# Weight preparation in half pieces, q written per half block, and the first attention block's loads moved: a two-layer streaming encoder on one core

## The chip, the core and the metric

The kernel runs on one core of a Trainium2 chip. The metric is the device time of one execution, in microseconds (us). The core has a matrix engine (TensorE, PE in the rows, with its weight loads as PEld), a vector engine (VectorE, DVE), an activation engine (ScalarE, ACT), a general engine (GpSimd, POOL) and a queue engine (SyncE, SP) that issues nearly all transfers. Each engine takes its instructions in the order in which they stand in its own queue, so an instruction that waits holds back all that stand behind it.

## What is computed

One inference step over 4096 prompt rows and 64 sample rows of width 1024: a gated convolution layer, then one shared key/value projection, then chunk-banded attention with sinks, each with RMS norms and residuals. Cut to what matters:

```python
# layer 0: z = rmsnorm(x) @ w_in + b; u = a * sigmoid(gl); c = depthwise conv31(u)
#          x1 = x + rmsnorm((silu(layernorm(c)) * silu(gate)) @ w_out + b_out)
kv = rmsnorm(x1, kv_g) @ w_kv                    # 2 heads of 64 for K and for V
z = rmsnorm(x1, b_pre_g) @ b_w_in                # 1024 q columns, 1024 gate columns
o = softmax(q @ K.T / 8 - slope * dist, sink) @ V    # own chunk of 64 and the two before it
y = x1 + rmsnorm((o * silu(gate)) @ b_w_out, b_post_g)
```

Each fp32 product is made of three fp16 products (high and low parts), accumulated in PSUM.

## The kernel before, in words

The program has four stages, in order of time.

1. **Stage A** (to about 1120 us): input projections of layer 0 and the depthwise convolution, in blocks of 512 rows.
2. **Output stage** (1120 to 1545 us): the loop `for ti in range(EARLY, len(L) + 1)` calls `la_iter(ti)`, a software pipeline over 33 tiles of 128 rows: layer norm, silu, gate, 48 matmuls with `w_oa`, and the rows of x1 to the DRAM scratch `x1_scr`. The first ten iterations stand in the stage before. On odd `ti` one weight job is called: two `kv_chunk`s and four `strassen_chunk`s that prepare the weights of q (`w_q...`). From `ti` 27 on, the steps of `prep_x1` for the first two blocks of the next stage are called in between.
3. **Projection stage** (1550 to 1998 us): 17 blocks of up to 256 rows in the order 0 to 14, 16 (the sample rows), 15. `proj_qkv(b)` gives ten PE jobs: the seven Strassen products of q in 128x128 tiles (`p1` to `p7`), K, and V twice. Between them stand the nine steps of `prep_x1` of the next block: norm, transposes, split into high and low parts, sums for the Strassen products (`tTb`). `out` adds up a product of q into an fp32 tile `zq`; when both halves (`th` 0 and 1) of 256 columns are there, `put_q` scales, splits and stores them in `q_scr`. From block 7 on (`G_AT`), odd blocks call one `strassen_chunk` for the gate weights and even blocks four `put_w_ob`.
4. **Attention stage** (from 1998 us): units of (128 rows, KV head). `load_att(b)` fetches q (`qraw`, then copied to `qs` on POOL), `ks` and `v_`. `gate_jobs(b)` are the seven Strassen products of the gate, popped by `filler` between the steps of the units; those of block 0 are called whole at the end of the projection stage.

`strassen_chunk(..., i)` (L865 to L898) loads 128 rows of 2048 values in two halves, 1 MB in four transfers of 256 KB into one buffer `wst`, scales them with two activations of 1024 columns, forms S1 to S4 on POOL (512 columns, L876), and splits seven operands: an ACT copy to fp16 (L883), a DVE subtraction for the low part (L884).

The order of instructions is not that of the code alone. The `TileContext` orders each engine's queue by a simulated timeline: when an engine is free in the simulation, it takes the earliest called instruction that is ready there. So a piece of work that is called late but needs little is put ahead, as early as its buffers allow. The tile constants `bias`, `sk` and `nsk` (L1343 to L1353) are made at the start of the attention stage, in its pool `pb`, which shares memory with the projection stage's pool `p3`.

Of the kernel before, what the change touches and what calls it, by code (L numbers as in the profile page):

```python
# [60 lines left out]
G_AT = 7  # L61
# [6 lines left out]
def tile_streaming_conformer(  # L68
# [778 lines left out]
    q_scr = dpool.tile([nb, 2, 2, P, 4, TB], F16, name="q_scr")  # L847
# [14 lines left out]

    OPS = ("A11", "S1", "S2", "A12", "S3", "A22", "S4")

    def strassen_chunk(pool, dst, names, base, i):  # L865
        st = pool.tile([P, 2, D], F32, tag="st", name="wst", bufs=1)
        src = ins["b_w_in"][0].rearrange("(g h kb c) n -> g c h kb n", g=4, h=2, c=G4)
# [4 lines left out]
        v = dict(A11=st[:, 0, 0:HN], A12=st[:, 1, 0:HN], A21=st[:, 0, HN:], A22=st[:, 1, HN:])  # L872

        def comb(name, a, b, op):
            v[name] = pool.tile([P, HN], F32, tag="sw", name=f"sw_{name}", bufs=3)
            nc.gpsimd.tensor_tensor(out=v[name], in0=v[a], in1=v[b], op=op)  # L876

        def put(name):
            if name in names:
                o = dst[name][:, :, i, :]  # L880
            else:
                o = pool.tile([P, 2, HN], F16, tag="wo", name=f"wo_{name}", bufs=1)
            nc.scalar.copy(o[:, 0], v[name])  # L883
            nc.vector.tensor_tensor(out=o[:, 1], in0=v[name], in1=o[:, 0], op=ALU.subtract)  # L884
            if name not in names:
                nc.sync.dma_start(out=wg_scr[OPS.index(name) - 5, :, :, i, :], in_=o)

        put("A11")
        put("A12")
        put("A22")  # L890
        comb("S1", "A21", "A22", ALU.add)
        put("S1")
        comb("S2", "S1", "A11", ALU.subtract)
        put("S2")
        comb("S3", "A11", "A21", ALU.subtract)
        put("S3")
        comb("S4", "A12", "S2", ALU.subtract)
        put("S4")  # L898
# [195 lines left out]
    def proj_qkv(b, ht, pool):  # L1094
# [4 lines left out]
        def put_k(src, n, scale, dst, name):  # L1099
            o = pool.tile([P, 2, TB], F16, tag="ko", name=name)  # L1100
# [46 lines left out]
        def put_q(kv, src):  # L1147
            zh = pool.tile([P, 4, TB], F16, tag="qo", name=f"qh_{b}_{kv}", bufs=4)
            zl = pool.tile([P, 4, TB], F16, tag="qo", name=f"ql_{b}_{kv}", bufs=4)
            for jj in range(4):  # L1150
                scale = SQ * 2.0 ** (4 * kv + jj) / 8.0 / SP
                nc.scalar.activation(zh[:, jj, :T], src[:, jj, :], AF.Copy, scale=scale)
                nc.vector.scalar_tensor_tensor(
                    out=zl[:, jj, :T], in0=src[:, jj, :], scalar=scale, in1=zh[:, jj, :T],
                    op0=ALU.mult, op1=ALU.subtract,
                )
            for z, t in ((0, zh), (1, zl)):
                nc.sync.dma_start(out=q_scr[b, kv, z, :, :, :T], in_=t[:, :, :T])

        if samp:  # L1160

            def q_half(half):
                ps = ps_mm([P, KH, CH], f"psqs_{half}")
                samp_half(wq, hT, tT, half, ps)
                put_q(half, ps)
# [3 lines left out]
        zq = {}  # L1169

        def out(nh, th, ps, add):
            if nh not in zq:
                zq[nh] = pool.tile([P, 4, TB], F32, tag="zq", name=f"zq_{b}_{nh}")
            dst = zq[nh][:, :, th * P : th * P + P]
            if add is None:
                nc.scalar.copy(dst, ps)
            else:
                nc.vector.tensor_tensor(out=dst, in0=ps, in1=add, op=ALU.add)
            zq[nh, th] = True
            if (nh, 0) in zq and (nh, 1) in zq:  # L1180
                put_q(nh, zq[nh])
# [5 lines left out]
    with ExitStack() as ph:  # L1187
# [11 lines left out]
        def kv_chunk(k0):  # L1199
            st = pl.tile([P, 4, 2 * P], F32, tag="st", name="wst", bufs=1)  # L1200
            split_weight(w_kv, ins["w_kv"], st, list(range(k0, k0 + 4)), 0, 256, 0, 1, quads=True)

        wjobs.extend(lambda k0=k0: kv_chunk(k0) for k0 in (0, 4))
        wjobs.extend(lambda i=i: strassen_chunk(pl, wq, OPS, 0, i) for i in range(KH))

        early = deque()
        for ti in range(EARLY, len(L) + 1):
# [10 lines left out]
            if ti % 2 == 1 and wjobs:  # L1218
                wjobs.popleft()()
        while wjobs:  # L1220
            wjobs.popleft()()
# [62 lines left out]

    with ExitStack() as ph:
# [4 lines left out]
        gjobs.extend(lambda i=i: strassen_chunk(p3, wg, OPS[:5], D, i) for i in range(KH))  # L1290
        wob_v = ins["b_w_out"][0].rearrange("(k p) n -> p k n", p=P)

        def put_w_ob(g, k):
            st = p3.tile([P, HN], F32, tag="wos", name=f"wob_{g}_{k}", bufs=1)
            nc.sync.dma_start(out=st, in_=wob_v[:, k, g * HN : g * HN + HN])
            w = p3.tile([P, 2, HN], F16, tag="wow", name=f"wobs_{g}_{k}", bufs=1)
            nc.scalar.activation(w[:, 0], st, AF.Copy, scale=SW)
            nc.vector.scalar_tensor_tensor(
                out=w[:, 1], in0=st, scalar=SW, in1=w[:, 0], op0=ALU.mult, op1=ALU.subtract
            )  # L1300
            nc.sync.dma_start(out=wob_scr[k // KH * 2 + g, :, :, k % KH, :], in_=w)

        ojobs = deque(lambda g=g, k=k: put_w_ob(g, k) for g in range(2) for k in range(KB))
# [3 lines left out]
        for q_, b in enumerate(order3):  # L1307
# [23 lines left out]
        assert not gjobs and not ojobs  # L1331
# [3 lines left out]
        for _, fn in gate_jobs(0):  # L1335
            fn()
# [3 lines left out]
    with ExitStack() as ph:  # L1340
        pb = ph.enter_context(tc.tile_pool(name="pb", bufs=2, reuse_waits="tile"))

        bias = pb.tile([P, 3 * CH], F32, tag="bias", name="bias", bufs=1)  # L1343
        nc.sync.dma_start(out=bias, in_=ins["alibi"])
        sk = pb.tile([P, 2, 4], F32, tag="sk", name="sk", bufs=1)
        sinks = ins["b_sinks"][0].rearrange("(a t s) -> s a t", a=2, s=2)
        for s_ in range(2):
            nc.sync.dma_start(out=sk[s_ * 64 : s_ * 64 + 64], in_=sinks[s_].partition_broadcast(64))
        nsk = pb.tile([P, 2, 4], F32, tag="nsk", name="nsk", bufs=1)
# [351 lines left out]
```

## Time and profile before

| | us |
|---|---|
| runs (3), median | 2980.38 (2977.71 to 2984.27) |
| the profiled execution | 2980.22 |
| its span, first to last instruction | 2978.1 |
| PE busy in the span | 2812.6 (94%) |
| DVE busy | 2340.3 (79%) |
| ACT busy | 1886.2 (63%) |
| POOL busy | 1830.6 (61%) |

A busy time is a sum over instructions of one engine; the engines work side by side, so the times don't add up. What a stage costs is read where PE, the busiest engine, is idle or has a low granted clock.

### The profile page before, as it was taken

To read this page: it belongs to the slowest core of one execution; us is meant where nothing else is said; L and a number is where in the kernel's file an instruction comes from. 1 tells how busy PE (TensorE), PEld (TensorE's weight loads), DVE (VectorE), ACT (ScalarE), POOL (GpSimd) and SP (SyncE) were. 2 spreads that over 40 slices of the span, in tenths; PEclk is the share of its full clock that TensorE was granted. 3 is DMA by queue.
4 is the path that set the end of the run, shared out by engine and by line. 5 is a ranking of instruction groups with operands and counts; after the bars stand their busy time and mean duration, and the time that the engine had idled before them with its cause. 6 is when DMAs were issued, how large, how long until landed. Compare 5 with 4: busy or idle time off the path is not lost.

```text
span 2978.1 us, 63632 instructions
## 1 busy us (share of the span) xinstructions
PE 2812.6 (94%) x24441; PEld 1795.0 (60%) x24441; DVE 2340.3 (79%) x4387; ACT 1886.2 (63%) x4403; POOL 1830.6 (61%) x1867
## 2 busy tenths in 40 slices
PE   8989999999999988988997899997999999999998
PEld 5444444444444433444457899996777777777774
DVE  6999899999999999979877767735666666666665
ACT  6787776877776675456667676634555555555554
POOL 7899899998898999978635433313323333332332
PEclk9999999999999999989999999999999999999999
DMA  5311211211110125576647655556323332432321
GB/s 182 110 48 38 74 50 43 66 48 46 47 40 29 50 90 171 162 194 191 190 159 236 218 200 187 180 162 202 99 92 115 113 99 92 130 100 92 111 81 47
DMA packets 250742, 341.25 MB, mean 115 GB/s; under 512 B 38886, under 2 KB 172774, under 8 KB 249670
## 3 DMA queue, kind: packets, MB, share of 16 engines
q1 hardware_dynamic: 250437, 337.19, 35.3%
q8 instruction: 191, 3.13, 0.5%
q14 instruction: 114, 0.93, 0.1%
HBM read 206.46 MB, written 130.72 MB: 113 GB/s over the span
## 4 chain that ended last, share of the span: by engine, by line
PE 37%; DVE 5%; ACT 3%; DMA 3%; issue 1%; POOL 1%; SPq 1%; POOLq 0%; DVEq 0%; ACTq 0%
PE sx_g L904 5%; PE sx_q L904 4%; PE psy L182 4%; PE psy L179 4%; PE psy L180 4%; PE sz_g L904 3%; PE ptr L1493 3%; PE pv L1527 3%; PE sz_q L904 2%; PE sw_g L904 1%; ACT p L1458 1%; PE sc L1427 1%; PE sc L1428 1%; PE sw_q L904 1%; DVE p L1431 1%
## 5 line engine op out<-in xcount | busy, mean ns | idle before, releaser
L597 POOL TENSOR_TENSOR pacc<-pacc,pr 128x512 f32<-128x512 f32 x704 | 907.4, 1304 | 69.7 <-ACT pr L588 42.6
L611 DVE SCALAR_TENSOR_TENSOR acc<-u,pt,acc 128x512 f32<-128x512 f32 x1088 | 789.4, 750 | 17.8
L588 ACT ACTIVATE pr<-u,pt 128x512 f32<-128x512 f32 x704 | 485.0, 715 | 162.0 <-POOL pacc L597 150.0
L1458 ACT ACTIVATE p<-p,st 128x192 f32<-128x192 f32 (+1 forms) x520 | 227.8, 440 | 76.2 <-DVE st L1452 75.9
L1431 DVE CUSTOM_DVE_ANT_0 p<-sc,bias 128x192 f32<-128x192 f32 (+1 forms) x520 | 160.5, 349 | 87.0 <-PE sc L1428 64.7
L179 PE MATMUL psy<-w_oa,hl 128*128 128x512 f16 x512 | 202.0, 395 | 6.0 <-DVE xr L392 4.9
L1477 POOL TENSOR_TENSOR p<-p,st 128x768 f32<-128x768 f32 (+2 forms) x130 | 185.5, 1447 | 34.5 <-DVE st L1473 27.8
L187 PE MATMUL ps_a<-hT,w_a 128*128 128x512 f16 (+1 forms) x528 | 198.2, 375 | 5.3 <-ACT sg L680 5.0
L187 PE MATMUL ps_gl<-hT,w_gl 128*128 128x512 f16 (+1 forms) x528 | 199.3, 377 | 3.8 <-ACT sig L751 1.9
L179 PE MATMUL psy<-w_ob,ogT 128*128 128x512 f16 x512 | 195.7, 382 | 7.0 <-ACT ogT L1543 6.8
L187 PE MATMUL ps_gt<-hT,w_gt 128*128 128x512 f16 x512 | 197.0, 385 | 5.4 <-DVE u L733 5.2
L180 PE MATMUL psy<-w_oa,hl 128*128 128x512 f16 x512 | 201.0, 393 | 0.0
L188 PE MATMUL ps_gl<-hT,w_gl 128*128 128x512 f16 (+1 forms) x528 | 199.3, 377 | 0.9 <-DVE hT L206 0.9
L189 PE MATMUL ps_gl<-hT,w_gl 128*128 128x512 f16 (+1 forms) x528 | 199.0, 377 | 0.0
L188 PE MATMUL ps_a<-hT,w_a 128*128 128x512 f16 (+1 forms) x528 | 198.0, 375 | 0.0
L189 PE MATMUL ps_a<-hT,w_a 128*128 128x512 f16 (+1 forms) x528 | 198.0, 375 | 0.0
L188 PE MATMUL ps_gt<-hT,w_gt 128*128 128x512 f16 x512 | 196.9, 385 | 0.0
L189 PE MATMUL ps_gt<-hT,w_gt 128*128 128x512 f16 x512 | 196.4, 384 | 0.0
L180 PE MATMUL psy<-w_ob,ogT 128*128 128x512 f16 x512 | 195.8, 382 | 0.0
L904 PEld LDWEIGHTS <-w_gS 128*128 128x128 f16 x3072 | 181.2, 98 | 20.2 <-issue 15.2
L904 PEld LDWEIGHTS <-w_qS 128*128 128x128 f16 x3072 | 177.3, 99 | 10.9 <-issue 10.5
L1377 POOL COPY qs<-qraw 128x1024 f16<-128x1024 f16 (+1 forms) x68 | 68.5, 1034 | 171.5 <-PE sc L1428 78.6
(352 smaller groups left out, 7079.9 us busy)
## 6 DMA issues: line engine op xcount, KB each, us to landing
x<-in_x_prompt SPq DMA_DIRECT2D x32, 512.0 KB, 3.8
g_scr<-sg SPq DMA_DIRECT2D x64, 256.0 KB, 2.2
c_scr<-c SPq DMA_DIRECT2D x64, 256.0 KB, 2.0
c<-c_scr SPq DMA_DIRECT2D x32, 512.0 KB, 4.2
g<-g_scr SPq DMA_DIRECT2D x32, 512.0 KB, 4.6
x<-x_scr SPq DMA_DIRECT2D x128, 128.0 KB, 3.6
h_scr<-hTb SPq DMA_DIRECT2D x32, 512.0 KB, 3.2
h_scr<-tTb SPq DMA_DIRECT2D x32, 512.0 KB, 3.7
```

The source lines that it names most:

```text
L179: nc.tensor.matmul(out, wts[i][0], mov[i][0], start=i == 0, stop=False)
L180: nc.tensor.matmul(out, wts[i][0], mov[i][1], start=False, stop=False)
L187: nc.tensor.matmul(out, wh, mh, start=i == 0, stop=False)
L188: nc.tensor.matmul(out, wh, ml, start=False, stop=False)
L189: nc.tensor.matmul(out, wl, mh, start=False, stop=i == n - 1)
L588: nc.scalar.activation(dst[:, :T], u[:, k : k + T], AF.Identity, scale=wdw[:, j, k : k + 1], bias=pt[:, j, R_DWB : R_DWB + 1] if k == 0 el ...
L597: nc.gpsimd.tensor_tensor(out=pacc[:, :T], in0=pacc[:, :T], in1=dst[:, :T], op=ALU.add)
L611: nc.vector.scalar_tensor_tensor(out=dst[:, :T], in0=u[:, k : k + T], scalar=wdw[:, j, k : k + 1], in1=src[:, :T], op0=ALU.mult, op1=ALU.add,)
L904: nc.tensor.matmul(ps[:, j, :], w[:, wz, kb, j * P : j * P + P], rhs(rz, kb), start=first and j + kb + wz + rz == 0, stop=last and j == KH ...
L1431: nc.vector.tensor_tensor_reduce(out=pbuf[:, t, par * 192 + lo : par * 192 + 192], in0=ps[:, tt, :nk], in1=bias[:, lo:], scale=1.0, scalar ...
L1458: nc.scalar.activation(pp, pp, AF.Exp, scale=2.0 ** -(kv * 4 + t) / SQ, bias=st[:, 1, par, t : t + 1], accum_out=st[:, 3, par, t : t + 1],)
L1477: nc.gpsimd.tensor_tensor(out=pp, in0=pp, in1=st[:, 4, par, :, None].to_broadcast([P, 4, 3 * CH - lo]), op=ALU.mult)
```

## The change

- `strassen_chunk` takes half of the columns (`hc`), so there are 8 pieces instead of 4 for q and 8 instead of 4 for the gate. It returns two functions, `load` and `comp`. A load is eight transfers of 64 KB. For q (`base` 0) the activations that scale a piece are four of 256 columns, and the factor 2^j of each 128 columns is folded in there (`gq`).
- In the output stage, an iteration calls either a `load` or the `comp` of the load before, in turn, from `ti` 10 on: ten pieces take the iterations 10 to 29. In the projection stage, a load of the gate weights is called after each of the blocks 2 to 9 in order (`G_AT = 2`) and one of `w_ob` after each of the first 16; the `comp`s are called after the next block.
- `queued()` puts each instruction of a `comp` on ACT, DVE and POOL behind the last instruction that was called on that engine before.
- `out` and `put_q` work on one product of 128 rows: the sum is left in PSUM, one activation and one DVE instruction of 512 columns split it, and the stores wait for both halves as before, in another layout of `q_scr`. The tile `zq` is gone.
- `load_att`, `bias`, `sk`, `nsk`, `unsc` move to a pool `stp` that is open during the projection stage as well. `load_att(0)` is called after the sample block, one block before the stage ends; the constants are made before the stage's first block. POOL copies q in eight pieces per block, not four.
- `gate_jobs(0)` is called after the first unit's scores and softmax statistics, not before the attention stage.

```diff
-G_AT = 7
+G_AT = 2
+    def queued():
+        es = ExitStack()
+        for e in (nc.scalar, nc.vector, nc.gpsimd):
+            seen = (x for x in reversed(nc.cur_bb.bb.instructions) if x.engine == e.engine)
+            es.enter_context(tc.issue_after(next(seen)))
+        return es
-    def strassen_chunk(pool, dst, names, base, i):
-        st = pool.tile([P, 2, D], F32, tag="st", name="wst", bufs=1)
-        for g in range(4):
-            nc.sync.dma_start(out=st[g * G4 : g * G4 + G4], in_=src[g, :, :, i, base : base + D])
-        for h in range(2):
-            nc.scalar.activation(st[:, h], st[:, h], AF.Copy, scale=gsc[:, 2, KH * h + i : KH * h + i + 1])
+    def strassen_chunk(pool, dst, names, base, i, hc):
+        def load():
+            box["st"] = st = pool.tile([P, 2, 2, HC], F32, tag="st", name="wst", bufs=1)
+            for g in range(4):
+                for h in range(2):
+                    s2 = src[g, :, h, i, base : base + D].rearrange("c (m n) -> c m n", m=2)
+                    nc.sync.dma_start(
+                        out=st[g * G4 : g * G4 + G4, h], in_=s2[:, :, hc * HC : hc * HC + HC]
+                    )
...
-        def put_q(kv, src):
-            for jj in range(4):
-                scale = SQ * 2.0 ** (4 * kv + jj) / 8.0 / SP
-                nc.scalar.activation(zh[:, jj, :T], src[:, jj, :], AF.Copy, scale=scale)
-                nc.vector.scalar_tensor_tensor(
-                    out=zl[:, jj, :T], in0=src[:, jj, :], scalar=scale, in1=zh[:, jj, :T],
+        def put_q(kv, th, src):
+            scale = SQ * 2.0 ** (4 * kv) / 8.0 / SP
+            nc.scalar.activation(zh, src, AF.Copy, scale=scale)
+            nc.vector.scalar_tensor_tensor(out=zl, in0=src, scalar=scale, in1=zh, op0=ALU.mult, op1=ALU.subtract)
...
-            if add is None:
-                nc.scalar.copy(dst, ps)
-            else:
-                nc.vector.tensor_tensor(out=dst, in0=ps, in1=add, op=ALU.add)
+            src = ps
+            if add is not None:
+                src = add if (nh, th) == (1, 1) else ps
+                nc.vector.tensor_tensor(out=src, in0=ps, in1=add, op=ALU.add)
+            put_q(nh, th, src)
...
-            if ti % 2 == 1 and wjobs:
-                wjobs.popleft()()
+            if wnext:
+                with queued():
+                    wnext.pop()()
+            elif wjobs:
+                load, comp = wjobs.popleft()
+                load()
+                wnext.append(comp)
...
-            if q_ >= G_AT and q_ % 2 and gjobs:
-                gjobs.popleft()()
+            while wnext:
+                with queued():
+                    wnext.pop()()
+            for js, at in ((ojobs, 0), (gjobs, G_AT)):
+                if js and q_ >= at:
+                    load, comp = js.popleft()
+                    load()
+                    wnext.append(comp)
             if q_ == nb - 2:
+                load_att(0)
                 gate_load(0)
-            if q_ >= G_AT and q_ % 2 == 0 and ojobs:
-                for _ in range(4):
-                    ojobs.popleft()()
-        for _, fn in gate_jobs(0):
-            fn()
...
-        load_att(0)
         sc, stats = att_scores(*units[0])
         for fn in sc:
             fn()
         stats()
+        for _, fn in gate_jobs(0):
+            fn()
```

## Rows read from the trace of the kernel before

**Rows 1.** The page: PE's busy tenths in 40 slices of the span.

```profile
PE   8989999999999988988997899997999999999998
```

**Rows 2.** Four stretches: start:end, length, busy us and count per engine, clock, DMA.

```profile
1280.00:1430.00 150.00, 130.22 (x587) 61.55 (x586) 133.82 (x158) 98.29 (x204) 125.67 (x141) 0.93 0.67 188
1430.00:1500.00 70.00, 70.00 (x348) 35.13 (x346) 56.09 (x73) 42.55 (x95) 41.65 (x63) 1.00 0.61 186
1550.00:1736.00 186.00, 157.18 (x2472) 151.10 (x2473) 141.24 (x258) 129.67 (x350) 79.84 (x56) 0.95 0.68 217
1736.00:1932.00 196.00, 196.00 (x3307) 193.83 (x3305) 137.36 (x290) 136.77 (x411) 64.64 (x48) 1.00 0.53 184
```

**Rows 3.** Waits of ACT from 1280 to 1430: us in total, times, longest.

```profile
ACT w_qS L883 <- POOL sw_S L876: 12.3, 5, 4.1
ACT wst L871 <- DMA wst<-in_b_w_in: 10.7, 2, 6.5
```

**Rows 4.** Waits of ACT from 1550 to 1736.

```profile
ACT wobs L1297 <- DMA wob<-in_b_w_out: 12.7, 8, 4.8
```

**Rows 5.** DVE by line, 1280 to 1430: the subtractions of the weight jobs.

```profile
L884 DVE TENSOR_TENSOR w_qS<-sw_S,w_qS 128x512 f16<-128x512 f32 x16 | 16.1, 1015 | 0.0
L884 DVE TENSOR_TENSOR w_qA<-wst,w_qA 128x512 f16<-128x512 f32 x12 | 13.5, 1155 | 2.8 <-ACT w_qA L883 2.8
L159 DVE SCALAR_TENSOR_TENSOR w_kv<-wst,gsc,w_kv 128x256 f16<-128x256 f32 x8 | 5.5, 714 | 0.2 <-ACT w_kv L158 0.2
```

**Rows 6.** The tile wst: ns min/median/max; the last line is its transfers' landing.

```profile
L869 SPq DMA_DIRECT2D wst<-in_b_w_in x32: 323/423/798, 1301.1 to 1631.8; - x32
L871 ACT ACTIVATE wst<-wst,gsc x16: 1131/1135/1150, 1311.5 to 1639.3; 128x1024 f32<-128x1024 f32 x16
L876 POOL TENSOR_TENSOR sw_S<-wst x16: 1261/1390/1720, 1313.8 to 1643.5; 128x512 f32<-128x512 f32 x16
L883 ACT CAST w_qA<-wst x12: 600/606/618, 1314.5 to 1389.4; 128x512 f16<-128x512 f32 x12
DMA to landing us min/median/max: 2.6/5.2/10.2
```

**Rows 7.** The tile zq: the instructions that write q.

```profile
L1152 ACT ACTIVATE qh<-zq x128: 398/404/422, 1584.9 to 1997.6; 128x256 f16<-128x256 f32 x128
L1153 DVE SCALAR_TENSOR_TENSOR ql<-zq,qh x128: 410/419/1484, 1585.3 to 1998.1; 128x256 f16<-128x256 f32 x128
L1178 DVE TENSOR_TENSOR zq<-sz_q,U_q x32: 675/682/693, 1579.0 to 1995.8; 128x512 f32<-128x512 f32 x32
L1176 ACT COPY zq<-sx_q x16: 566/579/585, 1583.2 to 1993.1; 128x512 f32<-128x512 f32 x16
```

**Rows 8.** Timelines around an undisturbed block's start: start us, us, engine, line.

```profile
1806.14 2.96 DVE L1028 TENSOR_TENSOR tTb<-tf,tTb 128x256 f16<-128x256 f32 x6
...
1809.39 2.85 PE L904 MATMUL sx_q<-hTb,w_qA 128*128 128x128 f16 x48
...
1812.26 0.94 PE L904 MATMUL sz_q<-tTb,w_qS 128*128 128x128 f16 x14
```

**Rows 9.** Timelines of DVE, SP and PE at the start of attention; brackets: idle before.

```profile
1999.42 1.35 SPq L1348 DMA_DIRECT2D sk<-in_b_sinks  x2
...
2011.87 0.58 DVE L1352 TENSOR_SCALAR nsk<-sk 128x1 f32<-128x1 f32 x8 [13.35 <-DMA qraw<-q_scr]
2012.36 0.69 DVE L1274 TENSOR_TENSOR sw_g<-sw_g,P_g 128x512 f32<-128x512 f32 x1
...
2014.21 4.46 PE L904 MATMUL sx_g<-tl,w_gA 128*128 128x128 f16 x48 [7.43 <-ACT U_g L922]
...
2027.34 0.49 PE L904 MATMUL sx_g<-tl,w_gS 128*128 128x128 f16 x6 [1.23 <-DMA tl<-h_scr]
...
2034.14 4.19 PE L904 MATMUL sx_g<-tl,w_gS 128*128 128x128 f16 x43 [2.68 <-ACT U_g L922]
```

**Rows 10.** Transfers by tile: count, KB each, median us from issue to landing.

```profile
x<-x_scr SPq DMA_DIRECT2D x128, 128.0 KB, 3.6
...
wst<-in_w_kv SPq DMA_DIRECT2D x8, 128.0 KB, 8.7
```

More of the change, by code (lines that the diff above doesn't have):

```diff
@@ L861, in tile_streaming_conformer @@
         nc.gpsimd.tensor_copy(fv[:, g], fv[:, 0])
+    gq = cpool.tile([P, 4, KB], F32, name="gq")
+    for j in range(4):
+        nc.gpsimd.tensor_scalar(gq[:, j], gsc[:, 2], scalar1=2.0**j, scalar2=None, op0=ALU.mult)
     OPS = ("A11", "S1", "S2", "A12", "S3", "A22", "S4")
-    def strassen_chunk(pool, dst, names, base, i):
-        st = pool.tile([P, 2, D], F32, tag="st", name="wst", bufs=1)
-        src = ins["b_w_in"][0].rearrange("(g h kb c) n -> g c h kb n", g=4, h=2, c=G4)
-        for g in range(4):
-            nc.sync.dma_start(out=st[g * G4 : g * G4 + G4], in_=src[g, :, :, i, base : base + D])
-        for h in range(2):
-            nc.scalar.activation(st[:, h], st[:, h], AF.Copy, scale=gsc[:, 2, KH * h + i : KH * h + i + 1])
[L872 to L880, printed above, removed]
-            else:
[L882 to L898, printed above, removed]
@@ L1099, in put_k @@
         def put_k(src, n, scale, dst, name):
-            o = pool.tile([P, 2, TB], F16, tag="ko", name=name)
+            o = pool.tile([P, 2, TB], F16, tag="ko", name=name, bufs=1)
             nc.scalar.activation(o[:, 0, :n], src, AF.Copy, scale=scale)
@@ L1199, in kv_chunk, with load @@
         def kv_chunk(k0):
[L1200 to L1204, printed above, removed]
+            box = {}
+            def load():
+                st = pl.tile([P, 4, 2 * P], F32, tag="st", name="wst", bufs=1)
+                box["f"] = split_weight(
+                    w_kv, ins["w_kv"], st, list(range(k0, k0 + 4)), 0, 256, 0, 1, now=False, quads=True
+                )
+            return load, lambda: box["f"]()
+        wjobs.extend(kv_chunk(k0) for k0 in (0, 4))
+        wjobs.extend(strassen_chunk(pl, wq, OPS, 0, i, hc) for i in range(KH) for hc in range(2))
+        wnext = []
         early = deque()
@@ L1283, in tmp @@
         return stp.tile([P, KH, P], F32, tag=tag, name=name)
+    bias = stp.tile([P, 3 * CH], F32, tag="bias", name="bias", bufs=1)
+    nc.sync.dma_start(out=bias, in_=ins["alibi"])
+    sk = stp.tile([P, 2, 4], F32, tag="sk", name="sk", bufs=1)
+    sinks = ins["b_sinks"][0].rearrange("(a t s) -> s a t", a=2, s=2)
+    for s_ in range(2):
+        nc.sync.dma_start(out=sk[s_ * 64 : s_ * 64 + 64], in_=sinks[s_].partition_broadcast(64))
+    nsk = stp.tile([P, 2, 4], F32, tag="nsk", name="nsk", bufs=1)
@@ new lines, in tile_streaming_conformer, with load_v @@
+    unsc = stp.tile([P, 2, 4], F32, tag="unsc", name="unsc", bufs=1)
+    for t in range(8):
+        nc.vector.tensor_scalar_mul(nsk[:, t // 4, t % 4 : t % 4 + 1], sk[:, t // 4, t % 4 : t % 4 + 1], -SQ * 2.0**t)
+        nc.gpsimd.memset(unsc[:, t // 4, t % 4 : t % 4 + 1], 2.0**-t / SQ)
+    vt = {}
+    def load_v(key, src, n):
+        v = vt[key] = stp.tile([P, 3, 2, P], F16, tag="v", name=f"v_{key}", bufs=4)
+        nc.sync.dma_start(out=v[:n, 0], in_=src)
+        for half in range(2):
+            hs = slice(half * 64, half * 64 + 64)
+            nc.sync.dma_start(out=v[hs, 1], in_=src[0:64])
+            if n > CH:
+                nc.sync.dma_start(out=v[hs, 2], in_=src[64:128])
@@ L1341, in tile_streaming_conformer @@
         pb = ph.enter_context(tc.tile_pool(name="pb", bufs=2, reuse_waits="tile"))
[L1343 to L1349, printed above, removed]
@@ L1350, in tile_streaming_conformer @@
-        unsc = pb.tile([P, 2, 4], F32, tag="unsc", name="unsc", bufs=1)
-        for t in range(8):
-            nc.vector.tensor_scalar_mul(nsk[:, t // 4, t % 4 : t % 4 + 1], sk[:, t // 4, t % 4 : t % 4 + 1], -SQ * 2.0**t)
-            nc.gpsimd.memset(unsc[:, t // 4, t % 4 : t % 4 + 1], 2.0**-t / SQ)
-        vt, U, OG = {}, {}, {}
-        def load_v(key, src, n):
-            v = vt[key] = pb.tile([P, 3, 2, P], F16, tag="v", name=f"v_{key}", bufs=4)
-            nc.sync.dma_start(out=v[:n, 0], in_=src)
-            for half in range(2):
-                hs = slice(half * 64, half * 64 + 64)
-                nc.sync.dma_start(out=v[hs, 1], in_=src[0:64])
-                if n > CH:
-                    nc.sync.dma_start(out=v[hs, 2], in_=src[64:128])
@@ L1399, in tile_streaming_conformer @@
+        U, OG = {}, {}
         pgb = pb.tile([P, D], F32, tag="pgb", name="pgb", bufs=1)
```

176 lines of the change are left out of this document (114 added, 62 removed).

## Prediction

> **What bounds the kernel now.** I read PE's line in 40 slices first [rows 1]: beside the first and the last slices it falls below 9 in four places: slices 15 and 16 (1042 to 1191 us, before the change's first instruction), 18 and 19 (the output stage, 1266 to 1415), 22 and 23 (the projection stage's first third, 1563 to 1712) and 28 (the start of attention). Elsewhere PE is nearly full, so the last three can give time. Then I counted what the dips cost with the busy times of four stretches [rows 2], by the number of matmuls done and not by the busy share, because a matmul at the low clock also counts as busy.
>
> In the output stage the stretch without weight jobs does 348 matmuls in 70 us, 4.97 per us, at clock 1.00. The 150 us before it, in which the q weights are prepared, do 587, worth 118.1 us at that pace: **31.9 us lost**, with clock 0.93. In the projection stage the undisturbed stretch does 3307 in 196 us, 16.87 per us (eight blocks of 24.5 us); the first six blocks, where the gate weights and `w_ob` are prepared, do 2472 in 186 us, worth 146.5: **39.5 us lost**. So the weight jobs called from block 7 on run in blocks 0 to 5: they were put ahead, into places where their engines looked free. At the start of attention [rows 9] PE stands idle 7.43, 1.23 and 2.68 us, and after two of these the first group runs at half the clock: 4.46 us for 48 matmuls against 2.85 [rows 8], and 4.19 for 43 against 2.55, so 3.2 more: **14.6 us lost**. Together 86.0 us.
>
> Why PE waits there: ACT stood 10.7 us on the landing of the q weights and 12.3 us on POOL's sums [rows 3], in the projection stage 12.7 us on `w_ob` rows [rows 4], each time with the copies that PE needs queued behind. Loads and the work on them were called together; a load takes 5.2 us to land, up to 10.2 [rows 6].
>
> **The change part by part.**
>
> *Weight pieces in the output stage.* A load now has an iteration's lead. An iteration is 54 matmuls (48 with `w_oa`, six short ones), 10.9 us at 4.97 per us. Issuing eight transfers costs SP 8 x 0.423 = 3.4 us [rows 6]; with the median landing of 5.2 that is 8.6 us, inside the iteration. So ACT's wait for loads should go. What is late next is DVE. Undisturbed it is busy 56.09 of 70 us [rows 2], so it has 2.17 us free per iteration, 43 us in the 20 iterations of ten pieces. The work is 16.1 + 13.5 + 5.5 = 35.1 us [rows 5]; halving adds 28 times 2 x 0.419 - 0.682 = 0.16, 4.4 us (durations of 256 and 512 columns, [rows 7]). That makes 39.5 of 43. It fits, but with no room, and the stretch that is undisturbed now gets its share. POOL's sums stretch DVE's subtractions too (means of 1.015 and 1.155 us against 0.68 alone [rows 5, 7]), which halves don't cure. I leave half of the loss in place and take **15 us gained** (some 1.8 us lost per half piece still, 17 us in all). Bounds: a loss of 3 (the same loss, and halves dearer) to a gain of 28.
>
> *Weight pieces in the projection stage.* One gate piece per block in blocks 3 to 10, one `w_ob` piece in each. ACT: two scalings of half 1.135 and seven copies of 0.404, 4.0 us; DVE seven of 0.419, 2.9 us alone; POOL four of half 1.39, 2.8 us [rows 6, 7]. A block leaves ACT 24.5 x (1 - 136.77/196) = 7.4 us and DVE 7.3 [rows 2]. Work fits, so what counts is lateness: the pieces stand ahead of the next block's preparation. Its last subtraction ends at 1809.10 and the first matmuls that read it start at 1812.26 [rows 8], so the chain has 3.2 us to give, against 4.0. I take 1.2 us lost per gate piece (9.6) and 0.1 for each of 16 `w_ob` pieces: of 39.5, **28 us gained**, bounds 5 to 37. The loads stand in SP's queue ahead of x1 loads and q stores and wait until the piece before is read; those have a block's lead, so nothing, at most 3 us, within the bounds.
>
> *q per half block.* Per block ACT goes from 0.579 + 8 x 0.404 = 3.81 to 4 x 0.579 = 2.32 us; DVE saves 8 x 0.419 - 4 x 0.682 = 0.6 us [rows 7]. In undisturbed blocks PE is the bound and this gives nothing; in the disturbed ones it is part of the 28. A PSUM tile of a product is now held over two more instructions, 1.3 us; the pool has a third tile, and no row shows PE waiting for one. Cost nothing; without that cover 0.7 us a block, 12 in all.
>
> *Start of attention.* The 7.43 us wait goes back to DVE, which stood 13.35 us on `nsk` until the sinks landed: issued at 1999.42, `nsk` at 2011.87, 12.4 us [rows 9]. Behind it stood the sum of a gate product, behind that ACT's copy, behind that PE. With constants and q of block 0 there a block earlier, and the first unit's softmax behind the gate products, the 14.6 us should go. I take **13 us gained**: the eight loads and eight POOL copies of `load_att(0)` now stand in SP's queue ahead of the last gate weights and the last block's stores, and two of the six `big` buffers are held in block 0. Bounds 5 to 14.6.
>
> *The sinks at their new place.* The transfer is the same and still lands 12.4 us after its issue; `nsk` now waits at the start of the projection stage, where block 1's transposes and the first sums stand behind it on DVE, and the x1 loads of block 1 behind the transfer on SP's queue. No row shows how early memory is free for it. Bounds: 12.4 us lost (DVE comes to it at once) to nothing (issued two iterations earlier); I take **6 us lost**, halfway, as nothing is nearer.
>
> Sum: 15 + 28 + 13 - 6 = 50. The profiled execution took 2980.22, 2.1 over its span and 0.16 below the median of three; 2980.2 - 50 = **2930 us**.
>
> **Rivals.**
>
> *The loss goes with the work.* Each half piece costs half of what a piece cost, so the 71.4 us stay and only 13 - 6 = 7 us come: 2973 us. For it speaks that the same instructions collide with the same neighbours and that DVE has no room in the output stage; against it that 23.4 us of ACT's waits [rows 3, 4] are for loads, which now come early.
>
> *The loads come late.* 64 KB transfers could land as slowly as the slowest now: 3.4 + 10.2 = 13.6 us against an iteration of 10.9, so ACT stands 2.7 us in each of ten iterations, 27 us: 2957 us. The rows lean both ways: 128 KB of x1 land in 3.6 us, 128 KB of `w_kv` in 8.7 [rows 10]. The Trainium skill speaks against this edit (DMA: Bandwidth & Descriptors, section Bandwidth): batch transfers to 1 MiB, since small ones spend their time on descriptors; by it this rival would come first. Its figures are for another issuing path, and the x1 row doesn't bear it out.
>
> *The pieces are free.* Both stages run at their undisturbed pace: 86 - 6 = 80 us, 2900 us. DVE's 39.5 of 43 us speaks against it.
>
> *Slower.* A piece stands whole ahead of the next iteration or block, because its instructions are called earlier: ACT scales (4 x 0.404), waits for POOL's four sums (2.8) as in [rows 3], copies 0.404, DVE 0.419, 5.2 us, and 0.6 for PE's low clock after it, 5.8 us. The 80 us that can be had are used up at 5.0 us for each of 16 half pieces; at 5.8 the time is 2980 - 80 + 93 = 2993 us. Against it: an undisturbed block has 3.2 us of slack, and ACT can take other work between two copies.
>
> That the change does nothing is hardly open: the order that it forces is on the very engines that made PE wait.
>
> **How the numbers follow.** Forecast (2910 to 2955) 0.62; free 0.09; late loads 0.09; loss with the work 0.13; slower 0.07. A measurement of this kernel tells 0.2%, 6 us, from no change. Faster by more: 0.62 + 0.09 + 0.09 and half of 0.13 make 0.86; within 0.2%: 0.06; slower: 0.08. The range reaches past the free case and to just below the third rival: 2897 to 2972.
>
> **What would show it.** Right: matmuls per us near 4.7 from 1280 to 1500 and near 16 in blocks 1 to 10; no wait of ACT for `wst` or `wob`; no 7 us gap before the first gate group; the gate subtractions spread over blocks 3 to 10. Wrong: DVE idle for ten us before `nsk` around 1550 with PE idle behind it; ACT waiting for `sw_S` in every piece; a gap in front of the first scores. The prediction falls if a half piece still costs PE above 3 us, or if the wait for the sinks costs more at its new place than at its old one.

## The result, and the profile after

| | before | changed |
|---|---|---|
| median of the runs, us | 2979.98 (2977.71 to 2984.27) | 2956.06 (2950.06 to 2958.04) |
| span of the profiled execution, us | 2978.1 | 2956.3 |
| ratio of the times, 95% interval | | 0.9915 (0.9896 to 0.9933) |

The kernel is 24 us faster, inside the range and well short of the 50 us that the sum gave. The first view is the one of [rows 2] again: busy times of the same four stretches (start:end, length, busy us and count of PE, its weight loads, DVE, ACT and POOL, clock, DMA share, GB/s).

```profile
1280.00:1430.00 150.00, 139.18 (x654) 66.53 (x652) 132.04 (x172) 96.44 (x222) 116.11 (x154) 0.98 0.64 195
1430.00:1500.00 70.00, 64.98 (x314) 31.21 (x313) 60.61 (x85) 50.59 (x128) 46.72 (x69) 1.00 0.54 165
1550.00:1736.00 186.00, 172.14 (x2858) 168.84 (x2856) 124.92 (x254) 123.54 (x344) 66.44 (x62) 0.97 0.64 208
1736.00:1932.00 196.00, 187.23 (x3109) 183.00 (x3107) 139.05 (x277) 138.64 (x387) 74.77 (x64) 1.00 0.64 209
```

Against [rows 2] the first stretch does 67 matmuls more and the second 34 fewer: the pieces are spread over the whole output stage, and half of what the disturbed stretch won is paid in the one that had none. In the projection stage it is the same, 386 more and 198 fewer.

ACT's waits for the loads of `wst` and `wob` are gone from 1280 to 1850 us. Its wait for POOL's sums, 12.3 us in five waits in [rows 3], is not; it comes in each of the eight q pieces (waits of ACT from 1280 to 1545: us in total, times, longest):

```profile
ACT w_qS L912 <- POOL sw_S L905: 18.6, 12, 3.7
```

To see where the 21.8 us between the two spans came from, I cut both spans at the same pieces of work: the first K matmul of projection blocks 0, 1, 2, 5, 6 and the last one, and the first value matmul of attention blocks 1, 9 and 15. PE's timeline of the changed kernel (start us, us, engine, line, operation):

```profile
1547.36 0.27 PE L187 MATMUL psk<-hTb,w_kv 128*128 128x256 f16 x1
...
1583.03 0.27 PE L187 MATMUL psk<-hTb,w_kv 128*128 128x256 f16 x1
...
1609.63 0.27 PE L187 MATMUL psk<-hTb,w_kv 128*128 128x256 f16 x1
...
1683.24 0.27 PE L187 MATMUL psk<-hTb,w_kv 128*128 128x256 f16 x1
...
1709.85 0.27 PE L187 MATMUL psk<-hTb,w_kv 128*128 128x256 f16 x1
...
1952.97 0.27 PE L187 MATMUL psk<-hTb,w_kv 128*128 128x256 f16 x1
...
2071.35 0.28 PE L1591 MATMUL pv<-pT,v_(1, 0)_24763 128*64 128x256 f16 x2
...
2541.57 0.28 PE L1591 MATMUL pv<-pT,v_(9, 0)_32051 128*64 128x256 f16 x2
...
2894.37 0.28 PE L1591 MATMUL pv<-pT,v_(15, 0)_37595 128*64 128x256 f16 x2
```

The same places (first and last K matmul, blocks 1, 9 and 15) in the kernel before:

```profile
1555.44 0.27 PE L187 MATMUL psk<-hTb,w_kv 128*128 128x256 f16 x1
...
1972.68 0.27 PE L187 MATMUL psk<-hTb,w_kv 128*128 128x256 f16 x1
...
2101.51 0.28 PE L1527 MATMUL pv<-pT,v_(1, 0)_24609 128*64 128x256 f16 x2
...
2567.16 0.28 PE L1527 MATMUL pv<-pT,v_(9, 0)_31865 128*64 128x256 f16 x2
...
2913.91 0.27 PE L1527 MATMUL pv<-pT,v_(15, 0)_37385 128*64 128x256 f16 x1
```

| from, to | before | changed | gain |
|---|---|---|---|
| start to the first K matmul (output stage's end) | 1555.4 | 1547.4 | 8.1 |
| to the last block's K matmul (projection stage) | 417.2 | 405.6 | 11.6 |
| to attention block 1 (start of attention) | 128.8 | 118.4 | 10.4 |
| to attention block 15 | 812.4 | 823.0 | **-10.6** |
| to the end | 64.2 | 61.9 | 2.3 |

The fourth line is a loss in a stage that the change hardly touches: of these 14 blocks it alters only the layout of q and the number of POOL's copies of it, and they take 0.8 us more each on average. And inside the projection stage the changed kernel's block 0 takes 35.7 us (1547.36 to 1583.03), the next 26.6, an undisturbed one 24.4. Block 0 holds the wait that the prediction had named as its own refutation. From the waits of PE and from DVE's and SP's timelines (brackets: idle before, and its releaser):

```profile
PE psv L187 <- DVE x L1044: 8.9, 1, 8.9
```

```profile
1551.10 1.34 SPq L1333 DMA_DIRECT2D sk<-in_b_sinks  x2
...
1563.37 0.58 DVE L1337 TENSOR_SCALAR nsk<-sk 128x1 f32<-128x1 f32 x8 [11.38 <-DMA sk<-in_b_sinks]
```

As in [rows 9], the sinks take about 12 us to land and DVE stands 11.38 us; what stood behind it there was a gate product, here it is block 1's transposes, and PE waits 8.9 us for them. The 7.43 us gap in front of the first gate group is gone: from the last K matmul to attention block 1, PE's waits for `U_g` fall from 10.1 to 0.7 us, while its waits for the loads of the gate operand (`tl`, `hl`) grow from 1.2 to 2.7.

### The profile page after: what moved, and what is told of

Its sections match the earlier page's. It is cut to its first block, busy times and chain, and to the rows that moved or that the text cites. A ratio compares the mean times of both kernels' runs of the same rounds, so it can differ in the third digit from the quotient of the medians.

```text
span 2956.3 us, 63971 instructions
## 1 busy us (share of the span) xinstructions
PE 2803.8 (95%) x24441; PEld 1788.6 (61%) x24441; DVE 2322.2 (79%) x4373; ACT 1885.9 (64%) x4405; POOL 1833.2 (62%) x1967
## 2 busy tenths in 40 slices
DMA packets 260601, 341.30 MB, mean 115 GB/s; under 512 B 40549, under 2 KB 184677, under 8 KB 259525
## 3 DMA queue, kind: packets, MB, share of 16 engines
q1 hardware_dynamic: 260293, 337.20, 35.7%
## 5 line engine op out<-in xcount | busy, mean ns | idle before, releaser
L179 PE MATMUL psy<-w_oa,hl 128*128 128x512 f16 x512 | 197.3, 386 | 1.0 <-DVE c L611 1.0
L180 PE MATMUL psy<-w_oa,hl 128*128 128x512 f16 x512 | 197.5, 386 | 0.0
L1371 POOL COPY qs<-qraw 128x512 f16<-128x512 f16 (+1 forms) x132 | 75.1, 614 | 136.7 <-PE sc L1492 76.5
```

Source lines behind the costliest of these rows:

```text
L179: nc.tensor.matmul(out, wts[i][0], mov[i][0], start=i == 0, stop=False)
L180: nc.tensor.matmul(out, wts[i][0], mov[i][1], start=False, stop=False)
```

## The experiments

Theory: the sum's terms, with three sizes open: the sinks' wait (at either place), DVE in the output stage, the start of attention. Rivals: that the transfers are late; that the forced order is worth nothing; that the loss in the attention blocks belongs to the pieces that still run in the last projection block.

**The sinks earlier, in both kernels** (`e1`, `e2`). The transfer is called in the first stage, with nothing that holds it back.

```
+            load_sinks()          # behind load_gains(), block 2 of the first stage
-    sk = stp.tile(...) ; two dma_start(out=sk[...]) ahead of nsk
```

> The changed kernel with one edit: the two transfers of the sinks are issued in stage A, at its third block, into a constant tile; nsk is still made at the start of the projection stage. Theory (the sinks' wait): the 11.4 us that DVE stands on nsk go, with them PE's 8.9 us wait for the transposes behind it and the half-clock group after it (4.28 against 2.84 us), so 2956 - 10 = 2946 us (2942 to 2949). Rival (block 1's preparation is late anyway: its x1 loads stand behind gate weights in the transfer queue): the wait only changes its name, 2953 us or more.

> The kernel before with the same one edit (sinks issued in stage A). Theory: the 13.35 us wait of DVE on nsk at the start of attention goes and with it PE's 7.4 us and 1.6 us of low clock: 2980 - 9 = 2971 us (2968 to 2974). Rival: something else is late there (q of block 0, the first scores), so that the softmax of the first unit ends when it did: 2978 us or more.

Measured: 2955.59 us, ratio 0.992 (0.9902 to 0.9938), no faster than the changed kernel; and 2977.32, ratio 0.9991 (0.9982 to 1.0001), no faster than the kernel before. In place, the theory held: the projection stage took 397.0 us instead of 405.6, and in the other kernel the stretch from the last K matmul to the end 995.3 instead of 1005.4. In that other kernel, where nothing but the sinks moved, the stretch from the last K matmul (1981.68 us) to attention block 1 (2100.70 us) took 119.0 us, against 128.8 before and 118.4 in the changed kernel. But the first K matmul came at 1555.1 instead of 1547.4 us, and at 1563.2 instead of 1555.4. The built program issued the transfer not in the middle of the first stage but at the head of SP's queue, in front of the program's first loads; the five weight loads shown came 8.5 us later. SP's timeline, first in the changed kernel, then with the early sinks:

```profile
12.93 8.41 SPq L148 DMA_DIRECT2D wst<-in_a_w_in  x5
```

```profile
3.62 3.38 SPq L117 DMA_DIRECT2D sk<-in_b_sinks  x2
...
21.42 8.36 SPq L155 DMA_DIRECT2D wst<-in_a_w_in  x5
```

The first stage's stretch shows the loss, in the same order:

```profile
0.00:1050.00 1050.00, 1008.46 (x5322) 490.02 (x5323) 981.77 (x1395) 771.41 (x1270) 954.04 (x831) 0.99 0.18 62
```

```profile
0.00:1050.00 1050.00, 1002.19 (x5287) 487.79 (x5288) 974.37 (x1386) 766.00 (x1262) 946.28 (x825) 0.99 0.18 62
```

PE is busy 6.3 us less there and does 35 matmuls fewer (in the kernel before 22 fewer, 5309 to 5287: some 5 of its 7.8 us; where the others went stays open). So this edit only moved the price: in the projection stage DVE waits for the transfer, at the head of the queue the first loads stand behind it, and some 8 to 12 us are lost around it in each place where it stood. Whether it would cost nothing in a place with room, such as 400 to 1050 us, where the DMA share is 0.13 in the changed kernel, no run shows.

**The same, with the gate operand loaded ahead of the first attention block's operands** (`e3`): two lines swapped.

```
+                gate_load(0)
                 load_att(0)
-                gate_load(0)
```

> As e1, and gate_load(0) called ahead of load_att(0) after the sample block. Theory (transfers collide in the last block): the gate's hl lands before the gate products that stand in the last block's PE queue, so PE's two waits for it (1.7 and 1.0 us) and the low clock behind them (some 3 us) go: 5 us less than e1, 2941 us. Rival: hl lands late because of the bytes ahead of it, not of its place, or the first scores become late instead: within 2 us of e1.

Measured: 2953.15 us, ratio 0.9911 (0.9894 to 0.9927); 2.4 us from `e1`, less than the runs of either spread over, and from the last K matmul to the end 1002.2 against 1001.3. The order of these loads carries nothing that can be told.

**The sinks in one transfer of 64-byte packets** (`e5`).

```
-    for s_ in range(2):
-        nc.sync.dma_start(out=sk[s_ * 64 : s_ * 64 + 64], in_=sinks[s_].partition_broadcast(64))
+    nc.sync.dma_start(out=skr, in_=ins["b_sinks"][0].partition_broadcast(P))
+    for s_ in range(2):
+        nc.vector.tensor_copy(sk[hs], skr[hs].rearrange("p (a t s) -> p s a t", a=2, s=2)[:, s_])
```

> The changed kernel, but the sinks come in one transfer of 128 packets of 64 bytes (all 16 values to each partition) and two small DVE copies put them where the 1024 packets of 4 bytes had put them; everything else stays. Theory: the 1024 packets of 4 bytes cost their 11 us wherever they stand, because loads of later blocks wait behind them (block 0 of the projection stage takes 35.7 us against 26.6 for the next). Then block 0 takes about 26 us, nsk waits under 4 us, and the time is 2944 to 2949 us. Rival: the wait for the sinks covers waits for the other loads of block 0 (its x and the next blocks' x1), which then stand last: block 0 at 32 us or more and 2952 to 2957 us.

Measured: 2947.4 us, ratio 0.9888 (0.9873 to 0.9903). Block 0 takes 26.4 us, the projection stage 394.0. SP's and DVE's timelines:

```profile
1549.59 0.42 SPq L1332 DMA_DIRECT2D skr<-in_b_sinks  x1
...
1552.49 0.35 DVE L1335 COPY sk<-skr 64x8 f32<-64x8 f32 x2 [2.01 <-DMA skr<-in_b_sinks]
```

2.9 us from issue to use instead of 12.3. The sizes of the transfers, in the changed kernel and here (KB of one):

```profile
sk<-in_b_sinks SPq DMA_DIRECT2D x2, 2.0 KB
```

```profile
skr<-in_b_sinks SPq DMA_DIRECT2D x1, 8.0 KB
```

Twice the bytes in a quarter of the time. What the page counts as packets under 512 bytes falls by 912, from 40549 to 39637: the sinks had come as 1024 packets of 4 bytes, since their index runs differently in memory and in the tile, and now come as 128 of 64. The trace's list of packets has 1040 fewer of 4 bytes and 128 new ones of 64, which makes the 912. This is the term of the sinks, shown: 11.6 us in the stage (405.6 to 394.0), 8.7 us in the medians.

**No queueing** (`e4`): the pieces are issued as before, wherever their engines look free; halves, lead and everything else stay.

```
-                with queued():
-                    wnext.pop()()
+                wnext.pop()()
```

> The changed kernel without queued(): half pieces, loads one step ahead, but the work on them may be put ahead of what was called before. Theory A (the order does it): pieces are drawn together again, ACT and DVE meet them in a clump and half of what the two stages gained is lost: 2966 us or more. Theory B (the lead of the loads does it, the order is idle): 2956 us within 4. Theory C (the forced order is what keeps the pieces dear, because they stand ahead of the next block): faster, 2950 us or less.

Measured: 2979.34 us, ratio 1.0001 (0.9991 to 1.001). The whole gain is gone. The first eight projection blocks take 38.4 to 28.6 us, and the stage 440.3; waits of PE from 1545 to 1800 (us in total, times, longest):

```profile
PE sx_q L935 <- ACT U_q L953: 26.9, 10, 6.0
```

ACT's copy of a finished product stands behind a gate piece. So the pieces are put ahead when nothing holds them back, and the queueing is what the projection stage gains by. The equal total hides two shifts: the projection stage alone is 34.7 us longer than in the changed kernel and 23.1 longer than before, and 9.7 us less from the last K matmul to the end (993.6 against 1003.3) make up for part of it; that part comes up again below.

**Queueing in the projection stage alone** (`e6`): the same edit in the output stage only.

> The changed kernel, but the weight pieces of the output stage are issued as they were before (not put behind the instructions already in the queues); the projection stage keeps the queueing. Theory: in the output stage DVE is full, and putting the pieces behind whole blocks gains nothing there, as the run without any queueing ended the output stage at 1535 us against 1542: the stage ends at 1535 to 1536 us and the time is 2949 to 2951 us. Rival: those 6.5 us came from the projection pieces no longer standing in the queues, or are taken back in block 0 of the projection stage: the first projection block starts at 1547 as before and the time is 2954 to 2957 us.

Measured: 2957.66 us, ratio 0.9924 (0.9911 to 0.9937), the first K matmul at 1547.5 us. My expectation fell: I had taken `e4`'s output stage to end 6.5 us earlier, but its first K matmul (1545.1 against 1547.4) shows only 2.3. In the output stage the queueing neither gains nor costs anything that can be told.

**No lead** (`e11`): loads and computation of a piece in the same slot.

```
-                load()
-                wnext.append(comp)
+                wnext.append(lambda load=load, comp=comp: (load(), comp()))
```

> The changed kernel, but a piece's loads are issued in the same place as its computation, one slot later than now, so that the half pieces and the queueing stay and the lead is gone. Theory: ACT, with a whole block queued behind the piece's first instruction, waits for the load (8.7 us from issue to landing for 128 KB in the worst row of before, 3.6 us in others): 2 to 6 us in each of eight pieces of the output stage's ten and in each of eight gate pieces, hence 2975 to 3010 us. Rival: the loads are issued early anyhow, because SP runs ahead of the other engines by about a block, and the lead is worth nothing: 2953 to 2959 us.

Measured: 2958.78 us, ratio 0.9935 (0.992 to 0.995), 2.7 us more than with the lead. The theory fell, the rival held. ACT's waits for the loads from 1280 to 1850, and the landing of the tile `wst`:

```profile
ACT wst L900 <- DMA wst<-in_b_w_in: 3.3, 2, 2.9
```

```profile
DMA to landing us min/median/max: 1.9/2.5/11.3
```

SP runs ahead of the other engines and issues the loads early in any case: those of the piece that ACT scales from 1384.0 us on were issued from 1379.10, and with the lead from 1375.60 for 1384.2. The transfers, now of 64 KB, land in 2.5 us at the median where those of 256 KB took 5.2 [rows 6]. So most of what the prediction gave to the lead isn't the lead's. In the projection stage it is the queueing's (`e4`); what the smaller loads bring by themselves is not shown, as no run changes their size alone.

**DVE's share taken away** (`e10`).

```
-                nc.vector.tensor_tensor(out=o[:, 1], in0=v[name], in1=o[:, 0], op=ALU.subtract)
+                nc.scalar.copy(o[:, 1], v[name])
```

> The changed kernel, but the low parts of the sixteen half pieces of w_q and w_g are written by an ACT copy instead of the DVE subtraction: the rounding that the low part stands for is left out of the computation. This takes 36 us of DVE work out of the output stage (56 subtractions, 36.2 us busy) and 3.2 us out of each gate piece, and gives ACT as many copies of 0.40 us. Theory: DVE has no room in the output stage, so that its time is on the path there: the first projection block starts 6 us or more earlier than at 1547.4, at 1541 or before. Rival: ACT and POOL, which prepare what DVE waits for, hold the stage: 1545 to 1548. For the gate pieces: if DVE is what they displace, their blocks go back to under 25 us; if ACT (busy 4.1 us per piece, then 6.9), they take 26 to 28 us. Time 2940 to 2950 us by the first, 2955 to 2965 us by the others.

Measured: 2948.71 us, ratio 0.9899 (0.9878 to 0.9921). The first K matmul comes at 1531.1 us, 16.3 earlier, so DVE's subtractions hold the output stage. The run doesn't part DVE from POOL: ACT's waits for POOL's sums fall with it from 18.6 to 7.5 us (1280 to 1545). The stretches to set beside those above:

```profile
1280.00:1430.00 150.00, 141.31 (x674) 69.49 (x673) 120.18 (x150) 111.09 (x270) 119.57 (x163) 0.98 0.67 203
1430.00:1500.00 70.00, 68.10 (x331) 33.12 (x329) 52.77 (x74) 57.70 (x155) 39.36 (x65) 1.00 0.60 181
```

In the projection stage neither expectation came out whole: five blocks with a gate piece take 25.0 to 26.3 us, three 29.1 to 32.3, and the stage 416.3. Waits of PE and of SP from 1640 to 1850:

```profile
PE tot L1023 <- ACT hTb L1018: 12.6, 7, 4.3
```

```profile
SPq L886 <- POOL sw_S L905: 27.9, 7, 5.8
```

SP stands at a piece's load until the piece before is read, and the next blocks' x loads behind it land late. In the changed kernel PE waits 2.0 us for `hTb` in that window. Which engine a gate piece displaces there stays open.

**The last six `w_ob` pieces two per block** (`e7`), so that none is left in the last three projection blocks.

```
+                if js is ojobs and q_ >= 10 and js:
+                    st2 = p3.tile([P, 2, HN], F32, tag="st", name="wob2", bufs=1)
+                    for j in range(2):
+                        load, comp = js.popleft()
+                        load(st2[:, j])
+                        wnext.append(comp)
```

> The changed kernel, but the last six of the 16 w_ob pieces go two per block behind blocks 10 to 12 instead of one per block behind blocks 10 to 15, so that none is left in the last three blocks. Theory: the last block and the start of attention lose about 10 us to the piece and its transfers that run in them (1003.3 us from the last block's first K matmul to the end, against 993.6 us where the pieces were done earlier): 994 to 996 us there, and 2946 to 2949 us in all. Rival: the 10 us lie with the loads of the first attention block and the gate operand, which stand in the last block either way: 1001 to 1004 us there and 2954 to 2958 us in all.

Measured: 2948.99 us, ratio 0.9898 (0.9883 to 0.9913); 7 us better than the changed kernel, but not where I expected it: 402.0 us in the projection stage (3.6 less) and 1000.3 from its last K matmul to the end (3.0 less, not 8). The 10 us that `e4` had gained there (993.6) were still unexplained.

**All three edits** (`e8`), and all three without one (`e9`: queueing in the output stage put back; `e12`: 4-byte sinks put back).

> The changed kernel with all three edits: sinks in 64-byte packets, queueing in the projection stage alone, the last six w_ob pieces two per block. Theory: three places on the path one behind the other, so the gains add up: 2956 - 9 - 6 - 9, 2930 to 2936 us. Rivals: they share a cause (the transfer queue around the start of the projection stage) and give less than the sum, 2940 to 2948 us; or none of them holds, 2952 to 2957 us.

> The run with all three edits, with the queueing in the output stage put back (sinks in 64-byte packets and w_ob pieces two per block stay). That queueing alone made no difference to the end of the output stage (1541.8 and 1542.0 us). But the compiled order of PE's instructions in the attention blocks is the one of the changed kernel here, and another one with all three edits, though the code of that stage is the same. Theory: the order costs the changed kernel about 1 us in each of blocks 9 to 14 and 8 to 10 us in all (59.4 against 58.4 us from block to block): those blocks take 59.4 us, and the time is 2943 to 2947 us. Rival: the last 10 us of the run with all three edits came from its three edits themselves: those blocks take 58.4 us and the time is 2934 to 2938 us.

> The run with all three edits, with the sinks' 4-byte packets put back (queueing in the projection stage alone and w_ob pieces two per block stay); the compiled order in the attention blocks is the faster one here. Theory (order and sinks add up): block 0 of the projection stage takes 36 us again, the attention blocks 9 to 14 take 58.4 us, and the time is 2942 to 2946 us. Rival (the order matters only with the early sinks, or not at all): 2948 us or more.

Measured: `e8` 2935.67 us, ratio 0.9851 (0.9838 to 0.9865), the fastest of all and 20 us under the changed kernel. Its 992.9 us from the last K matmul to the end were more than the edits explain, which led to the attention blocks. Their PE timeline in `e8`:

```profile
2058.88 0.28 PE L1602 MATMUL pv<-pT,v_(1, 0)_24762 128*64 128x256 f16 x2
...
2524.68 0.28 PE L1602 MATMUL pv<-pT,v_(9, 0)_32050 128*64 128x256 f16 x2
...
2873.14 0.30 PE L1602 MATMUL pv<-pT,v_(15, 0)_37594 128*64 128x256 f16 x2
```

465.8 and 348.5 us between them, against 470.2 and 352.8 in the changed kernel: 8.7 us, in code that is the same. What differs is the order in which the built program gives PE the instructions of a block. It is taken from the simulated timeline when the program is built, and comes out differently when something earlier differs. With all three edits, 43 matmuls of the gates stand in a row some 11 us into a block; the changed kernel has 21 of them there and 27 at the block's end, where they wait for ACT. One block, 10, of the changed kernel, its PE waits and its busy times:

```profile
PE sx_g L935 <- ACT U_g L953: 0.6, 1, 0.6
PE sc L1491 <- DVE mx L1495: 0.4, 1, 0.4
PE ptr L1557 <- POOL p L1541: 0.2, 1, 0.2
PE sx_g L935 <- ACT P_g L953: 0.2, 1, 0.2
```

```profile
2600.90:2660.30 59.40, 57.91 (x630) 42.33 (x628) 37.05 (x113) 32.22 (x104) 20.47 (x34) 1.00 0.32 103
```

and the same block with all three edits:

```profile
PE pv L1602 <- ACT pT L1576: 0.5, 1, 0.5
PE psy L179 <- ACT ogT L1618: 0.2, 1, 0.2
```

```profile
2583.10:2641.50 58.40, 57.72 (x628) 42.32 (x626) 36.70 (x115) 32.26 (x104) 20.54 (x34) 1.00 0.33 105
```

Four short waits of 1.4 us in all in place of two of 0.7, and the same four again in block 11. `e9` and `e12` test it: `e9` has two of the three edits, yet the changed kernel's order in these blocks; `e12` has 4-byte sinks and `e8`'s order. `e9` took 2940.6 us, ratio 0.9873 (0.9852 to 0.9893), with 470.3 and 352.8 us in those blocks; `e12` 2944.48, ratio 0.9883 (0.9868 to 0.9899), with 465.5 and 347.8. With `e7` this makes a square, all four with the early `w_ob` pieces (medians, us):

| | order of the changed kernel | order of `e8` |
|---|---|---|
| sinks in 4-byte packets | 2948.99 (`e7`) | 2944.48 (`e12`) |
| sinks in 64-byte packets | 2940.60 (`e9`) | 2935.67 (`e8`) |

The sinks give 8.4 and 8.8 us, the order 4.5 and 4.9: they add up. In the blocks themselves the order gives 8 to 9 us; 2.4 to 2.9 of it go back at the start, where block 0 takes 65.4 and 66.1 us in that order against 63.0 and 63.2. The two columns differ in the output stage's queueing as well, which by `e6` moves nothing there. All nine kernels with the one order (the changed one, `e1`, `e3`, `e5`, `e6`, `e7`, `e9`, `e10`, `e11`) took 59.3 to 59.4 us for blocks 10 to 13; `e4`, `e8` and `e12` with the other took 58.4 to 58.9, and the kernel before and `e2`, with a third, 57.8 to 58.7. POOL's eight copies of q are not the loss: `e4`, `e8` and `e12` have them too and take 813.3 to 814.3 us from block 1 to block 15, against 812.4 before and 823.0 in the changed kernel. That the loss in the attention blocks goes with the order is shown; what tips the order one way or the other stays open.

## Why the prediction was right and wrong

| term of the sum | predicted | measured | by |
|---|---|---|---|
| pieces in the output stage | 15 | 8.1 | first K matmul, 1555.4 to 1547.4 |
| pieces in the projection stage | 28 | 23.2 | 417.2 to 394.0 (`e5`, without the sinks' price) |
| q per half block | 0 | 0 | undisturbed blocks 24.4 us in both |
| sinks at the new place | -6 | -11.6 | 394.0 to 405.6 |
| start of attention | 13 | 10.4 | last K matmul to block 1, 128.8 to 118.4 |
| attention blocks 1 to the end | not in the sum | -8.3 | 876.6 to 884.9 |
| sum | 50 | 21.8 | spans: 21.8 |

- **The number**: every term that missed came out lower than predicted, so no error made up for another. 2956 us lies 1 us outside the 2910 to 2955 that had most of the chances, and 1 us from the 2957 of "the loads come late"; that nearness is chance, since ACT no longer waits for these loads.
- **Direction and mechanism** held: the three dips that the first view had singled out are where the time came from, and the order forced on the engines is what did it in the projection stage (`e4`: 1.0001 without it).
- **Output stage**: the step that failed is "I leave half of the loss in place". I had seen that DVE would be late next, with 39.5 us of work for 43 free, but took that as nearly fitting. It didn't fit: with 36.2 us of subtractions less the stage ends 16.3 us earlier (`e10`). And a sign that the prediction had named for being wrong came true, ACT waiting for `sw_S` in every piece, 18.6 us in all where there had been 12.3. Matmuls per us from 1280 to 1500 are 4.4 (968 in 220), not 4.7. The weight that the prediction gave to the lead was wrong too: `e11` loses 2.7 us without it, in all.
- **Gate pieces**: 1.2 us each were taken; their subtractions run in blocks 3 to 11, as the prediction's sign had it but for the last. Blocks 3 and 4 take hardly longer for it (24.45 and 24.72 us), 5 to 11 take 25.8 to 27.1 against 24.45, so 1.3 to 2.6 each, and 13.7 in these seven. With 64-byte sinks, blocks 0 and 1 keep 4.1 more that I had at nothing. The condition "above 3 us a half piece" wasn't met.
- **Sinks**: I took the middle of 0 and 12.4 because no row showed how early the transfer would be issued. It was issued 3.7 us behind the first K matmul, and DVE came to it at once: the lower bound. The prediction's own test, "if the wait for the sinks costs more at its new place than at its old one", is met within the noise: 11.6 us there, and 10.1 at the old place (1005.4 to 995.3, `e2`). Moving it was worth nothing in the places tried, changing its packets 8.7 us. What I missed is in [rows 9], where two transfers of 2 KB take 12.4 us to land while 128 KB land in 3.6 [rows 10]: the time couldn't be the bytes. The Trainium skill (DMA: Bandwidth & Descriptors, section Rules for kernel authors) says that under 64 KB a transfer is mostly overhead; the same page (section Specifications) wants 512 bytes or more to reach line rate. The first doesn't tell the two cases apart: 8 KB in 64-byte packets were in use 2.9 us after issue. The second points the right way, but both packets are far below it; what differs between the runs is their number, 1024 against 128.
- **Start of attention**: 10.4 of 13. That the wait for the sinks held PE there was right, but it is nearly all: `e2`, which moves the sinks alone, has 9.8 of the 10.4 us in this stretch (119.0 against 118.4). Loading q of block 0 earlier and calling the gate products later brought 0.6 us net beside that. So the move took about as much out of this stretch as it put into the projection stage, 10.4 and 11.6.
- **Not foreseen at all**: the 8.3 us in the attention blocks. The prediction costed only instructions that the diff touches, and took the order of all others as given.
- **Rivals**: "the loads come late" is refuted: ACT waits 3.3 us even without the lead, and smaller transfers landed sooner, so that the rule of the Trainium skill that the prediction had weighed for it (DMA: Bandwidth & Descriptors, section Bandwidth), which is about rate, is not borne out for the time that these loads take to land; "the loss goes with the work" holds in part, in the output stage; "the pieces are free" and "slower" did not come.

## What to carry to other kernels

A transfer that takes long for its bytes is to be looked at packet by packet before it is moved: here it cost about the same in each of the three places where it stood, and a fraction of that once it came in fewer packets. Where a moved instruction ended up is read from the trace, not from the place of its call. Work that fills in beside a busy stage needs an order that keeps it behind the work that the bound engine waits for, and the engine whose free time it was to fill almost to the end became the next bound here. Where a program's order is worked out when it is built, compare the untouched stages too, block by block: a small edit upstream can cost there what it gained in its own place.

## What was not expected of the hardware

1024 packets of 4 bytes, 4 KB in all, cost 8 to 12 us in each of three places of the program; in the first one nothing waited for their data yet, but the program's first loads stood behind them. And the smaller loads landed sooner: 128 transfers of 64 KB land in 2.5 to 2.6 us at the median, 32 of 256 KB took 5.2. SP has four times the issues, and with the lead ACT waits for none of these loads from 1280 to 1850 us. A piece's load is also half as many bytes as before, so that the size of a transfer by itself is not shown to be the cause.
